# A residual-stream kernel: first residual tiles early, one weight tile in front of the gated output's loads, post-processing on two engines

## The chip, the cores and the metric

The kernel runs on one core of one Trainium2 chip. A core has a matrix engine (PE, TensorE), a vector engine (DVE), an activation engine (ACT), a general engine (POOL, GpSimd) and a queue engine (SP) that here only issues transfers; ACT issues transfers too. Each engine works through its own instructions in order. Operands live in an on-chip memory of 128 partitions (SBUF), products land in eight accumulator banks (PSUM) of 128 x 512 float32, and everything larger lies in device memory (DRAM). The metric is the device time of one execution in microseconds (us), as the median of several runs.

## What is computed

The reference is a two-layer encoder trunk on a sequence of 1024 tokens with 1024 channels, all float32:

```
for layer in range(2):
    hn = rms_norm(h, mix_norm[layer])
    h = h + (hybrid_ab_mixer(hn) if layer == 0 else rwkv7_time_mix(hn))
    h = h + swiglu(rms_norm(h, ffn_norm[layer]))
return rms_norm(h, final_norm)

swiglu(x)     = (silu(x @ w_gate) * (x @ w_up)) @ w_down     # hidden width 2816 = 22 x 128
rwkv7 step    : state = state * w_t + (state a_t) b_t + v_t k_t ;  y_t = state r_t     # 16 heads of 64
rwkv7 output  : y = groupnorm(y) * ln_w + ln_b + bonus * v ;  return (y * g) @ w_o
```

The group norm is over each head's 64 channels. The recurrence is over time and is computed in 16 chunks of 64 tokens.

## The kernel before, in words

The 1024 tokens are worked as two halves of 512 (h = 0 and h = 1), with channels on partitions: a half of the residual stream, `H[h]`, is eight k-tiles of 128 x 512. Each float32 operand is split into a rounded part and a remainder, and one product becomes three matrix instructions (`mm3`, lines 391 to 393: high x high, high x low, low x high). A weight tile is loaded into one of three `raw` buffers (line 121, issued by ACT), split by ACT (line 157) and DVE (line 158), and used. The order of the weights is fixed in a list `plan`, filled by the `push` functions; `take(key)` takes the next entry, splits it, loads the two entries behind it and splits the one behind it.

Instructions are written in program order, and a planner then orders each engine's queue by its own model of time, taking what is ready by priority. Tiles get their place in SBUF from pools that are opened and closed like a stack from two ends, left and right. A tile placed over the bytes of closed pools waits, on its first use, for the last use of the tiles that lay there.

The parts that the change touches, in order of time:

*The first layer's down projection of half 0.* The first layer's feed-forward writes its hidden tiles to DRAM (`hid_d`, line 735). For the down projection (`down_steps`, line 875) they are read back (line 886) in groups of two and three hidden tiles; for each group and each of the eight output tiles m, PE sums the group's products in one bank, and DVE adds the bank to `H[h][:, m]` (`residual`, line 485). PSUM has five banks for these products there. `H[0]` was written to DRAM (`hm_d`) in the mixer and is loaded again (line 1856), four transfers of two k-tiles for each half. The even groups' weights and hidden tiles of half 0 lie in slots cut from two activation tiles (`low_slots`, line 1827), of which k-tiles 6 and 7 are not used.

*The first recurrence, with dense work beside it.* `recur` (line 1424) computes eight chunks of half 0. A chunk (`burst`, line 1552) is a sequence of blocks of 32 small products with short DVE and ACT steps in between: a first step for the next chunk (`below`, `below2`, `own`), the product with the state, the sum Q (line 1561), the product with Q, the state's update (lines 1590 and 1591) and the output `yp`. After each second chunk `post` (line 1615) normalises 128 tokens: it copies the outputs to `ysb`, takes statistics, applies scale and shift for each head (16 ACT instructions, line 1650), multiplies by `ln_w` and adds the bonus term, for the first half of the heads on DVE and for the second on POOL (lines 1655 and 1656). `turn_out` (line 1660) transposes `ysb` on PE, multiplies by the gate on DVE (line 1672) and writes the 128 tokens to `y_d` (line 1675, SP). `drive` interleaves this with half 1's feed-forward, whose last three down groups, hidden tiles 16 and 17, 18 and 19, 20 and 21 (`steps_b`, line 1897), stand behind it in program order. Their hidden tiles have four buffers in the feed-forward's pool, and the first two groups are loaded ahead (`prime_b(2)`).

*The output projection of half 0.* While the last down group is emitted, the four pieces of the gated output are taken from `y_d` (`take_act`, line 468; ACT issues the loads). Behind them in the plan stand the eight tiles of the output weights, each loaded by four transfers; `out_proj` (line 1698) takes them one by one, 24 matrix instructions each. In the same stretch the residual stream of half 1 is normalised (line 1075) and mixed for the second half's projections, on DVE and ACT; a low-rank and a gate product follow the output projection.

## Time and profile before

| what | value |
|---|---|
| median of 3 runs | 2505.56 us (2501.13 to 2507.78) |
| the profiled execution, its own time | 2500.52 us |
| its span, first to last instruction | 2498.8 us |
| mean granted clock of PE | 0.977 |
| busy: PE, DVE, ACT, POOL | 2365.3, 1481.1, 957.6, 237.3 us |
| moved by DMA | 346.38 MB, mean 139 GB/s |

A row of the timeline gives the start in us, the duration in us, the engine, the line of the kernel, the instruction, output <- inputs by the program's names, the count of merged instructions, and in brackets how long the engine had been idle and what released it. PEld is PE's weight load, which runs under the products. SPq and ACTq are the issue of transfers, not their duration. The clock is the share of full speed that PE was granted. Matrix instructions are pipelined, so that a row's duration is longer than the distance to the next.

### The profile page before, as it was taken

What the parts mean: (1) busy time and instruction counts of PE and PEld (TensorE: products, weight loads), DVE (VectorE), ACT (ScalarE), POOL (GpSimd) and SP (SyncE); (2) the same over time, 40 slices, a digit from 0 to 9 for tenths busy, and PEclk for the clock granted to TensorE, in tenths of its full rate; (3) what the DMA queues carried; (4) which work ended last, traced back from release to release, by engine and by line L of the source; (5) the groups of instructions that cost most, each with busy time, mean ns of one, the idle gap of its engine ahead of it and who ended that gap; (6) DMA issues with size and microseconds to landing.
All of it is one profiled execution on the core that took longest, in us unless ns stands there. A gap on an engine that the chain in (4) does not pass through costs nothing. (4 is left out here: it accounts for less than half of the span.)

```text
span 2498.8 us, 38219 instructions
## 1 busy us (share of the span) xinstructions
PE 2365.3 (95%) x15519; PEld 1941.4 (78%) x15519; DVE 1481.1 (59%) x2340; ACT 957.6 (38%) x1479; POOL 237.3 (9%) x262
## 2 busy tenths in 40 slices
PE   8999999999899999989958999998999999999998
PEld 6888888888687778768846778777888778888887
DVE  6446775666467947756766847855554446444344
ACT  6233444344213644423434654432342224322223
POOL 0200000000000023301210123201110000000001
PEclk9999999999899999999978999998999999999999
DMA  5124533333765455774434465693534322433231
GB/s 175 50 68 139 159 129 120 120 120 118 251 222 206 153 165 141 217 211 134 142 128 124 145 170 140 186 238 109 142 110 143 108 80 74 152 100 114 90 95 57
DMA packets 419249, 346.38 MB, mean 139 GB/s; under 512 B 94656, under 2 KB 364096, under 8 KB 418304
## 3 DMA queue, kind: packets, MB, share of 16 engines
q10 hardware_dynamic: 264000, 193.75, 25.6%
q1 hardware_dynamic: 155072, 150.18, 19.6%
q8 instruction: 122, 2.00, 0.3%
q14 instruction: 55, 0.45, 0.1%
HBM read 264.11 MB, written 79.76 MB: 138 GB/s over the span
## 5 line engine op out<-in xcount | busy, mean ns | idle before, releaser
L391 PE MATMUL mm<-ahi,whi 128*128 128x512 f32 x1312 | 516.9, 395 | 22.8 <-ACT whi L157 21.6
L392 PE MATMUL mm<-alo,whi 128*128 128x512 f32 x1312 | 517.5, 394 | 0.1
L393 PE MATMUL mm<-ahi,wlo 128*128 128x512 f32 x1312 | 515.9, 393 | 1.4 <-DVE wlo L158 1.4
L157 ACT ACTIVATE whi<-raw 128x1024 fp32r<-128x1024 f32 (+1 forms) x276 | 274.1, 1000 | 581.6 <-PE mm L392 433.7
L158 DVE TENSOR_TENSOR wlo<-raw,whi 128x1024 fp32r<-128x1024 f32 (+1 forms) x276 | 321.9, 1169 | 213.8 <-ACT whi L157 200.8
L391 PEld LDWEIGHTS mm<-ahi,whi 128*128 128x128 f32 x1312 | 248.2, 189 | 78.9 <-ACT whi L157 24.3
L485 DVE TENSOR_TENSOR h<-h,mm 128x512 f32<-128x512 f32 x280 | 188.5, 684 | 194.4 <-PE mm L393 176.4
L393 PEld LDWEIGHTS mm<-ahi,wlo 128*128 128x128 f32 x1312 | 248.0, 189 | 55.2 <-DVE wlo L158 2.2
L392 PEld LDWEIGHTS mm<-alo,whi 128*128 128x128 f32 x1312 | 248.4, 189 | 54.2 <-issue 2.0
L391 PE MATMUL mm<-hidhi,wdhi 128*128 128x512 f32 x304 | 117.6, 397 | 5.8 <-ACT hidhi L947 2.8
L392 PE MATMUL mm<-hidlo,wdhi 128*128 128x512 f32 x304 | 119.6, 394 | 0.0
L393 PE MATMUL mm<-hidhi,wdlo 128*128 128x512 f32 x304 | 119.3, 392 | 0.0
L722 PE MATMUL mm<-ahi,whi 128*128 128x512 f32 x280 | 109.4, 391 | 0.0
L723 PE MATMUL mm<-alo,whi 128*128 128x512 f32 x280 | 109.0, 389 | 0.0
L724 PE MATMUL mm<-ahi,wlo 128*128 128x512 f32 x280 | 108.2, 389 | 0.0
L158 DVE TENSOR_TENSOR wdlo<-raw,wdhi 128x1024 fp32r<-128x1024 f32 x42 | 53.0, 1262 | 76.0 <-ACT wdhi L157 76.0
L157 ACT ACTIVATE wdhi<-raw 128x1024 fp32r<-128x1024 f32 x42 | 44.3, 1057 | 138.0 <-DMA raw<-in_ffn_w_down_dram 103.9
L944 DVE TENSOR_TENSOR sg<-sg,mm 128x512 f32<-128x512 f32 x48 | 32.9, 686 | 98.7 <-PE mm L393 98.6
L391 PE MATMUL mm<-hd,dhi 128*128 128x512 f32 x192 | 75.1, 391 | 4.1 <-DMA hd<-hid_d 2.6
L392 PE MATMUL mm<-hd,dhi 128*128 128x512 f32 x192 | 75.1, 391 | 0.0
L393 PE MATMUL mm<-hd,dlo 128*128 128x512 f32 x192 | 74.1, 389 | 0.0
L391 PEld LDWEIGHTS mm<-hidhi,wdhi 128*128 128x128 f32 x304 | 57.3, 189 | 20.8 <-DVE h L485 3.8
(395 smaller groups left out, 4457.2 us busy)
## 6 DMA issues: line engine op xcount, KB each, us to landing
raw<-in_ffn_w_down_dram ACTq DMA_DIRECT2D x88, 512.0 KB
raw<-in_ffn_w_gate_dram ACTq DMA_DIRECT2D x72, 512.0 KB
raw<-in_ffn_w_up_dram ACTq DMA_DIRECT2D x72, 512.0 KB
hid_d<-hid SPq DMA_DIRECT2D x40, 512.0 KB
hd<-hid_d SPq DMA_DIRECT2D x30, 512.0 KB
raw<-in_ab_w_in_dram ACTq DMA_DIRECT2D x16, 512.0 KB
raw<-in_ab_w_out_dram ACTq DMA_DIRECT2D x16, 512.0 KB
raw<-in_rwkv_w_r_dram ACTq DMA_DIRECT2D x16, 512.0 KB
```

What stands on the lines that cost most here:

```text
L157: act.activation(hi, src, AF.Copy)
L158: (eng or dve).tensor_tensor(out=lo, in0=src, in1=hi.bitcast(F32), op=ALU.subtract)
L391: pe.matmul(o, whi, xhi, start=first, stop=False)
L392: pe.matmul(o, whi, xlo, start=False, stop=False)
L393: pe.matmul(o, wlo, xhi, start=False, stop=last)
L485: dve.tensor_tensor(out=H[h][:, m, :], in0=H[h][:, m, :], in1=o, op=ALU.add)
L722: pe.matmul(o, wh[:, k, :], x[0][:, k, :], start=st, stop=False, skip_group_check=True)
L723: pe.matmul(o, wh[:, k, :], x[1][:, k, :], start=False, stop=False, skip_group_check=True)
L724: pe.matmul(o, wl[:, k, :], x[0][:, k, :], start=False, stop=k == 3, skip_group_check=True)
L944: dve.tensor_tensor(out=s, in0=s, in1=o, op=ALU.mult)
```

## The change

The change has three parts, all in program order and placement; the values computed are the same.

First, when the slots of `low_slots` are made, two transfers on SP load the first four k-tiles of `hm_d[0]` into the unused k-tiles 6 and 7 of both tiles. In the first down group of half 0 the add for m = 0 to 3 reads these tiles and writes `H[0]`; the loads into `H[0]` itself are now two instead of four. `H[1]` is loaded as before.

Second, the first tile of the output weights moves in the plan from behind the four pieces of the gated output to in front of them, and is taken first (`with_first`). An empty event keeps the places of the other work in that list. Along with it, half 1's hidden tiles 16 and 17 keep two buffers in the feed-forward's pool and are loaded ahead; tiles 18 to 21 get four buffers in a new pool `ffn1y`, opened on the left behind the gated output's tiles, after the recurrence's pool is closed.

Third, in `post` the scale and shift of the first half of the heads are two DVE instructions on 128 x 512 with broadcast operands instead of eight ACT instructions, and both halves' product with `ln_w` and sum with the bonus term run on DVE; the two POOL instructions are gone. This is in both recurrences, four times each.

```diff
--- before.py
+++ after.py
@@ -339,8 +339,10 @@
     for e in push_f(0, 1, D0P):
         e()
     push_d(0, 1, D0B[1])
+    o_first = push_o(0)
+    o_first[0]()
     list(push_act(("y", 0), y_d[0]))
-    push_beside(1, push_o(0) + push_f(1, 0, G1A[0]))
+    push_beside(1, [lambda: None] + o_first[1:] + push_f(1, 0, G1A[0]))
     push_proj(1, ("n1", n_d[1]))
     push_ffn(1, 0, G1A[1])
     push_ffn(1, 0, G1A[2], push_act(("y", 1), y_d[1]))
@@ -872,7 +874,7 @@
             go()
             yield 0.5
 
-    def down_steps(h, groups, wslot, hslot, ahead=True, after=None, between=iter(()), at={}):
+    def down_steps(h, groups, wslot, hslot, ahead=True, after=None, between=iter(()), at={}, first={}):
 
         held = {}
         for g in groups:
@@ -902,7 +904,10 @@
                     ms = slice(m * P, (m + 1) * P)
                     for i, f in enumerate(g):
                         mm3(o, wd[f][0][:, ms], wd[f][1][:, ms], held[f][:, 0, :], held[f][:, 1, :], i == 0, i == len(g) - 1)
-                    residual(m, h, o)
+                    if gi == 0 and m in first:
+                        dve.tensor_tensor(out=H[h][:, m, :], in0=first[m], in1=o, op=ALU.add)
+                    else:
+                        residual(m, h, o)
                     if after is not None and gi == len(groups) - 1:
                         after(m)
                     if gi == len(groups) - 1 and m % 2:
@@ -1644,16 +1649,17 @@
             rsqrt(var)
             dve.scalar_tensor_tensor(out=mean, in0=mean, scalar=-0.5, in1=var, op0=ALU.mult, op1=ALU.mult)
             yield 0.3
-            for r in range(2):
-                for p in range(8):
-                    i = r * 8 + p
-                    act.activation(
-                        ysb[:, r, p, :], ysb[:, r, p, :], AF.Identity, scale=var[:, i : i + 1], bias=mean[:, i : i + 1]
-                    )
+            vb, mb = (bc(t[:, 0:8].unsqueeze(2), [P, 8, 64]) for t in (var, mean))
+            for p in range(8):
+                act.activation(
+                    ysb[:, 1, p, :], ysb[:, 1, p, :], AF.Identity, scale=var[:, 8 + p : 9 + p], bias=mean[:, 8 + p : 9 + p]
+                )
+            dve.tensor_tensor(out=ysb[:, 0], in0=ysb[:, 0], in1=vb, op=ALU.mult)
+            dve.tensor_tensor(out=ysb[:, 0], in0=ysb[:, 0], in1=mb, op=ALU.add)
             yield 0.3
-            for q, eng in enumerate((dve, pool)):
-                eng.tensor_tensor(out=ysb[:, q], in0=ysb[:, q], in1=lnw, op=ALU.mult)
-                eng.tensor_tensor(out=ysb[:, q], in0=ysb[:, q], in1=vch[:, q], op=ALU.add)
+            for q in range(2):
+                dve.tensor_tensor(out=ysb[:, q], in0=ysb[:, q], in1=lnw, op=ALU.mult)
+                dve.tensor_tensor(out=ysb[:, q], in0=ysb[:, q], in1=vch[:, q], op=ALU.add)
             yield 0.3
 
             def turn_out():
@@ -1695,9 +1701,16 @@
         turned.pop()()
         yield 1.0
 
+    early_o = {}
+
+    def with_first(h):
+        early_o[h] = take(("o", h, 0))
+        yield from take_act(("y", h))
+
     def out_proj(h, ys, after=None):
         for m in range(KT):
-            yield from out_steps(take(("o", h, m)), ys, h, m, range(KT), after)
+            w = early_o.pop(h) if m == 0 and h in early_o else take(("o", h, m))
+            yield from out_steps(w, ys, h, m, range(KT), after)
 
     def turn(h, j):
 
@@ -1822,11 +1835,15 @@
     ps_es = open_psum("psf0", FULL)
     wp, wp_es = open_pool(name="wp", bufs=1, side="left")
 
-    low = []
+    low, first = [], {}
 
     def low_slots():
         if not low:
             low.extend(act_tiles(xlp))
+            for i, t in enumerate(low):
+                t = t[:, 6:8, :].bitcast(F32)
+                sp.dma_start(t, hm_d[0][:, 2 * i : 2 * i + 2, :])
+                first.update({2 * i + j: t[:, j, :] for j in range(2)})
         return [t[:, 2 * i : 2 * i + 2, :] for i in range(4) for t in low]
 
     lw = lambda f: [t.rearrange("p k t -> p (k t)") for t in low_slots()[2 * (f - D0A[[f in g for g in D0A].index(True)][0]) :][:2]]
@@ -1847,12 +1864,12 @@
     prime_b, steps_b = down_steps(1, D0B[0], wslot, hslot, False, lambda m: sp.dma_start(h_d[1, 0][:, m, :], H[1][:, m, :]))
     acc, add = running_sums(0)
     prime_a, steps_a = down_steps(
-        0, D0A, lambda f: (lw, wslot)[odd[f]](f), lambda f: (lh, hslot)[odd[f]](f), after=add, at={len(D0A) - 1: prime_b},
+        0, D0A, lambda f: (lw, wslot)[odd[f]](f), lambda f: (lh, hslot)[odd[f]](f), after=add, at={len(D0A) - 1: prime_b}, first=first,
     )
     prime_a()
     for h, pl in ((0, ha_pool), (1, hb_pool)):
         H[h] = pl.tile([P, KT, HT], F32, tag="h", name="h")
-        for k in range(0, KT, 2):
+        for k in range(4 * (1 - h), KT, 2):
             sp.dma_start(H[h][:, k : k + 2, :], hm_d[h][:, k : k + 2, :])
 
     def wa1():
@@ -1891,17 +1908,21 @@
     hb_pool, hb_es = open_pool(name="hb1", bufs=1, side="left")
     wp, wp_es = open_pool(name="wp0", bufs=1, side="left")
     f, f_es = open_pool(name="ffn1", bufs=1, side="right")
-    _, hslot = slots_of(f, 0, 4)
+    _, hslot = slots_of(f, 0, 2)
+    late = []
     spill_h = lambda m: sp.dma_start(h_d[1, 1][:, m, :], H[1][:, m, :])
     between = []
-    prime_b, steps_b = down_steps(1, D0B[1], lambda f: whl(), hslot, True, spill_h, (next(between[0]) for _ in range(4)))
-    prime_b(2)
+    prime_b, steps_b = down_steps(1, D0B[1], lambda f: whl(), lambda f: (hslot if f < 18 else late[0])(f), True, spill_h, (next(between[0]) for _ in range(4)))
+    prime_b()
     drive(ffn(0, 1, nxt["hn"], f, D0P, nd=2), with_reload(hb_pool, 1, h_d[1, 0], recur(0, wp)), 9.3)
     wp_es.close()
     y, y_es = open_pool(name="y0", bufs=1, side="left")
     ys = open_act(("y", 0), y)
-    between.append(take_act(("y", 0)))
+    fy, fy_es = open_pool(name="ffn1y", bufs=1, side="left")
+    late.append(slots_of(fy, 0, 4)[1])
+    between.append(with_first(0))
     drive(steps_b)
+    fy_es.close()
     f_es.close()
     ps_es.close()
     np_, np_es = open_pool(name="np1", bufs=1, side="right")
```

## The prediction, made before the changed kernel ran

> **What bounds the kernel now.** I read the page's engine shares first, then busy time by stretch, then what TensorE (PE) waited for, then the timeline around the two longest waits.
>
> ```profile
> span 2498.8 us, 38219 instructions
> PE 2365.3 (95%) x15519; PEld 1941.4 (78%) x15519; DVE 1481.1 (59%) x2340; ACT 957.6 (38%) x1479; POOL 237.3 (9%) x262
> ```
>
> PE is the bound: 133 us of the span are not PE's. No edit removes a matmul, so the change can only move PE's idle time. Stretches of the span (us, then PE, PEld, DVE, ACT, POOL busy with counts, granted clock, DMA share, GB/s):
>
> ```profile
> 624.00:636.00 12.00, 11.51 (x51) 9.13 (x50) 5.61 (x8) 4.70 (x7) 0.00 (x0) 1.00 0.98 353
> ...
> 655.70:666.90 11.20, 0.04 (x2) 0.04 (x1) 0.78 (x2) 0.00 (x0) 0.00 (x0) 0.64 0.82 271
> 666.90:673.70 6.80, 6.80 (x19) 5.38 (x20) 4.72 (x7) 0.75 (x1) 0.00 (x0) 0.59 1.00 404
> ...
> 1222.80:1278.50 55.70, 52.43 (x987) 44.08 (x985) 40.84 (x85) 21.43 (x44) 8.17 (x7) 1.00 0.42 131
> 1278.50:1323.10 44.60, 7.02 (x21) 4.35 (x20) 26.57 (x61) 19.06 (x36) 6.46 (x4) 0.56 0.41 130
> 1301.20:1370.00 68.80, 48.09 (x199) 39.09 (x200) 47.88 (x63) 34.82 (x49) 0.00 (x0) 0.81 0.54 159
> ```
>
> Two holes carry nearly half of the idle time: 11.2 us where the first half's down projection begins, and 37.6 us between the end of the first recurrence and the output projection. PE's waits in the second (total, times, longest):
>
> ```profile
> PE mm L391 <- ACT whi L157: 20.7, 2, 17.1
> PE sm L1451 <- DVE ysb L1656: 11.5, 1, 11.5
> ...
> PE sm L1451 <- ACT akv L1549: 1.4, 1, 1.4
> ```
>
> **The first hole: residual tiles.** PE fills its five accumulators and stops at 655.7; the residual add that would free one waits for H. SP's issues, PE, DVE, and what SP waited for:
>
> ```profile
> 623.41 0.32 SPq L886 DMA_DIRECT2D alo<-hid_d  x1
> ...
> 648.94 1.99 SPq L1856 DMA_DIRECT2D h<-hm_d  x4
> ...
> 659.67 1.74 SPq L1856 DMA_DIRECT2D h<-hm_d  x4
> 661.45 3.62 SPq L886 DMA_DIRECT2D hd<-hid_d  x3
> ```
>
> ```profile
> 666.87 0.80 PE L391 MATMUL mm<-ahi 128*128 128x512 f32 x1 [11.16 <-DVE h L485]
> ...
> 673.68 0.39 PE L391 MATMUL mm<-hd,dhi 128*128 128x512 f32 x1
> ...
> 685.92 0.39 PE L391 MATMUL mm<-hd,dhi 128*128 128x512 f32 x1
> ```
>
> ```profile
> 666.12 1.28 DVE L485 TENSOR_TENSOR h<-h,mm 128x512 f32<-128x512 f32 x2 [11.70 <-DMA h<-hm_d]
> ```
>
> ```profile
> SPq L1856 <- DMA hid_d<-hid: 7.4, 1, 7.4
> ```
>
> Which four loads at L1856 are H[0]'s? The second four: the add starts 6.4 us after 659.67, and these had waited 7.4 us for a hidden tile's write-out, whose space H[0] takes. The change reads the first four k-tiles from another place, loaded along with the first hidden tiles, near 623, but the add still writes into H[0], so it still needs that space, free at 659.7. So I let PE restart at 659.7 + 0.7 (one add) = 660.4, 6.5 us earlier. What is late next is the second group's hidden tiles, issued at 661.45 behind H[0]. Two loads (1.05 MB) fewer ahead of them are worth 2.6 us at the 404 GB/s of the stretch from 666.9, 3.9 us at the 271 of the one before. Bounds: 0 (they land as before, and the group starts at 673.68 again) and 6.5. I take **-5**, nearer the upper end, because at 673.68 PE waited for none of them. The two early loads fall in a stretch where DMA is 0.98 busy: 3 us more transfer there, in front of the down projection's weights, which PE first uses near 648.9 (30 products of 0.227 us, below, before 655.7). That gap hides it; without it, +3.
>
> **The second hole, as it is.** Rows of PE, ACT, DVE, POOL and SP in order:
>
> ```profile
> 1277.38 1.15 PE L1451 MATMUL yp<-uv,gt 128*64 128x64 f32 x31
> ...
> 1293.77 1.75 PE L1451 MATMUL sm<-ident,ysb 128*128 128x128 f32 x7 [3.35 <-POOL ysb L1656]
> 1295.32 1.70 PE L426 MATMUL aux<-small,nacc 128*128 128x1 f32 x8
> ...
> 1330.65 0.62 PE L393 MATMUL mm<-ahi,wlo 128*128 128x512 f32 x2
> ```
>
> ```profile
> 1285.63 5.41 ACT L1650 ACTIVATE ysb<-ysb,mean,var 128x64 f32<-128x64 f32 x16 [5.92 <-DVE mean L1645]
> 1300.42 1.30 ACTq L121 DMA_DIRECT2D raw<-y_d  x3
> 1304.40 2.25 ACT L157 ACTIVATE ahi<-raw 128x1024 fp32r<-128x1024 f32 x2 [13.36 <-DMA raw<-y_d]
> ```
>
> ```profile
> 1278.36 0.69 DVE L1591 TENSOR_TENSOR state_d<-Q,pct 128x512 f32<-128x512 f32 x1
> ...
> 1289.14 0.69 DVE L1656 TENSOR_TENSOR ysb<-ysb,vch 128x512 f32<-128x512 f32 x1
> ...
> 1301.21 4.70 DVE L1075 SCALAR_TENSOR_TENSOR hn<-h,vec,aux 128x512 f32<-128x512 f32 x7 [2.17 <-PE aux L439]
> ...
> 1316.23 1.22 DVE L158 TENSOR_TENSOR alo<-raw,ahi 128x1024 fp32r<-128x1024 f32 x1
> ```
>
> ```profile
> 1292.46 1.26 POOL L1656 TENSOR_TENSOR ysb<-ysb,vch 128x512 f32<-128x512 f32 x1
> ```
>
> The recurrence ends at 1278.5. Its last chunk pair is normalised (16 activations, then DVE, then POOL to 1293.7), turned, written and read back: y loads issue at 1300.42, the last of four pieces is split at 1317.5, and only then come the projection's first weights. Its first tile (m=0) is done at 1330.7.
>
> **Post-processing.** Activation's 16 become 8 x 0.34 = 2.7 us. DVE gets six passes of 0.72 (0.69 and the step between): two with a broadcast operand, which L1591 also has at 0.69. Four run while Activation works; the last two end 1285.6 + 4.3 = 1289.9, against POOL's 1293.7: **-3.9** in the tail. On the other seven chunk pairs DVE carries 2.9 us more each and Activation 2.7 less. Dense products hide it while PE has some; without them, +2.9 a pair if DVE's queue decides, -1.4 if Activation's does (the akv wait above). I take 0.
>
> **The late hidden tiles.** Tiles 18 to 21 now go to a pool in the space of the recurrence's tiles, so they load when it ends, and their 96 products can no longer run under it. Behind the waiting loads on SP stand the other half's spills and y's last write, all due later. How much of them ran there:
>
> ```profile
> L391 PE MATMUL mm<-hd,whi 128*128 128x512 f32 x33 | 13.6, 411 | 0.0
> ```
>
> 33 triples (99 products) after 1222.8: all of it. One product takes 0.227 us (54 from 673.68 to 685.92), so 21.8 us move from a stretch that is 94% busy into one that is 84% idle. What does the recurrence do without them? Its chunks (the product with Q, the next chunk's first step, and that step's bare sequence early on):
>
> ```profile
> 1108.35 0.69 PE L1451 MATMUL sm<-XT,gt 32*32 32x32 f32 x32
> ...
> 1111.53 0.98 PE L1451 MATMUL sm<-state_d,ar 64*64 64x64 f32 x27
> ...
> 1126.08 1.72 PE L1451 MATMUL sm<-Q,XT 64*64 64x64 f32 x32
> ```
>
> ```profile
> 1229.70 1.11 PE L1451 MATMUL sm<-Q,XT 64*64 64x64 f32 x32
> ...
> 1235.58 0.69 PE L1451 MATMUL sm<-XT,gt 32*32 32x32 f32 x32
> ...
> 1250.17 1.15 PE L1451 MATMUL sm<-Q,XT 64*64 64x64 f32 x32 [0.28 <-DVE Q L1561]
> ...
> 1273.43 1.15 PE L1451 MATMUL sm<-Q,XT 64*64 64x64 f32 x32
> ```
>
> The last two chunks took 20.5 and 23.3 us. Bare: 5.9 to the next step (1229.70 to 1235.58), 4.2 for it (1108.35 to 1112.5), about 1.2 for the add of Q: 11.3. I take 15.5, nearer the bare chain, since DVE and Activation still carry the post-processing. Two chunks give 12.8, the one before 2.2: the recurrence ends 15 us earlier, at **1263.5**. Bounds 0 and 21.8 (all of the products).
>
> Then, in order: the tiles land 4.0 after the release (as y did, 1300.42 to 1304.40), 1267.5; 96 products and 2.4 of transposes end at 1291.7. The y chain took 21.9 from the recurrence's end to its loads; now 18.0 and 1.0 for residual adds on the same DVE, 1282.5; plus 17.0 for the last split, 1299.5.
>
> **First weights in front.** Four DMAs on Activation's queue, one activation (1.05) and one DVE pass (1.22) move ahead of the y loads, under the last down products; uncovered, 2.3. The second weights take the place the first had. So m=0 runs as the pieces come, done 1.4 after the last: 1300.9 against 1330.7, **-29.8** with the two edits above.
>
> **What is late next.** The other half's norm needs the late groups' sums: 1291.7 + 2 + 5.9 (1295.32 to 1301.21) = 1299.6, hardly earlier than 1301.21. From there to 1370 DVE has 47.9 us of work, 43 without the y splits, now partly before; the projection's other seven tiles need 7 x 24 x 0.227 = 38.1 and end at 1339, but the low-rank and gate products want that DVE work, 1342.6. So about **+4**.
>
> Sum: -5 - 29.8 + 4 = -30.8. The profiled execution took 2500.52 (1.7 beside the span), the runs' median is 2505.56; off the median, **2474.8, so 2475**.
>
> **Rivals.**
>
> *The recurrence keeps its pace.* Thin PE work lets the clock fall: early on, at 1126.08, the product with Q took 1.72 instead of 1.11, as L391's took 0.80 after the first hole instead of 0.39. With eleven blocks of about 1 us a chunk, 0.55 each is 6 us: 15.5 becomes 21.5. Against it: 15.5 leaves only some 4.5 us of waits a chunk, spread over several places. If it comes, the recurrence ends at 1278.5, m=0 at 1316, the norm starts at 1314.6 and DVE holds the gate to 1357.6 instead of 1354: -14.7 + 4 - 5, 2490. The Trainium skill, "TensorE: Matmul & The Clock Gate", Part 1, has PE throttled only after about 3.4 us without work; by that rule this rival would not come, and the trace's clock of 0.64 in the 11.2 us hole agrees that long holes do it.
>
> *Slower: the late loads queue behind the y write-out.* SP works in order. If the four loads stand behind the last write of y, which cannot issue before 1293, and the recurrence keeps its pace, the groups run from 1297 to 1321 (2.4 more at half clock), the norm starts at 1331, and the gate's operands are there at 1331 + 48 = 1379 against 1369: +10 - 5, 2511. The planner issues what its own clock has ready, and the release comes 15 us before the write, which speaks against.
>
> *Everything at its bound.* Chunks at 11.3, 21.8 won, m=0 at 1294, +3.6 after, and -8 in front (6.5 and a shorter cold spell): 2464.
>
> *It doesn't do what it says.* A planned order that changes elsewhere by as much, or late tiles lying over space freed only by the post-processing: 2503.
>
> **Numbers.** Forecast 0.58, pace kept 0.16, at the bounds 0.12, nothing 0.07, slower 0.07. A measurement here tells about 0.3% (7.5 us) from no change: faster 0.85, same 0.08, slower 0.07. Range 2458 to 2498; the forecast's own 2464 to 2486.
>
> **What would show it.** PE restarting near 660 with the add no longer waiting for H; products on tiles 18 to 21 after the recurrence's last product and before the y loads' split; that last product near 1263 less the front's gain; transposes right behind DVE, not POOL; m=0 done some 30 us earlier against the same point, and a new wait for DVE before the gate. It is wrong if the recurrence ends as late as now, or if the loads of tiles 18 to 21 come after the last write of y.

## The result, and the profile after

The changed kernel takes 2478.39 us (median; 2476.45 to 2481.59) against 2503.97 for the kernel before: a ratio of 0.9905, 95% interval 0.989 to 0.992, or 25.6 us less. The profiled execution took 2477.8 us, its span 2476.1 against 2498.8. The head of the page and its engine shares:

```profile
span 2476.1 us, 38179 instructions
...
PE 2371.4 (96%) x15519; PEld 1948.0 (79%) x15519; DVE 1496.4 (60%) x2372; ACT 937.6 (38%) x1415; POOL 215.5 (9%) x246
```

PE's products are the same in number; its idle time went from 133.5 us to 104.7, and 6.1 us of that came back as longer products. DVE has 15 us more work, ACT 20 less, POOL 22 less. To see where the time went, the span is cut at two products that both kernels have. The first is the start of the second down group, 673.68 in the prediction's rows; the other is the first product of the second recurrence. The kernel before, timeline of PE:

```profile
1318.24 0.80 PE L391 MATMUL mm<-ahi,whi 128*128 128x512 f32 x1 [17.07 <-ACT whi L157]
...
1652.80 0.29 PE L1453 MATMUL sm<-ar,bk 64*64 64x128 f32 x1 [0.60 <-DMA bk<-bk_d]
```

The kernel after, the same products:

```profile
665.26 0.47 PE L393 MATMUL mm<-hd,dhi 128*128 128x512 f32 x1
...
1307.37 0.39 PE L393 MATMUL mm<-ahi,whi 128*128 128x512 f32 x1
...
1641.07 0.32 PE L1458 MATMUL sm<-ar,bk 64*64 64x128 f32 x1
```

Up to the second down group 8.4 us were won (673.68 - 665.26). From there to the second recurrence the two kernels take 979.1 and 975.8 us: 3.3 won, where the prediction had 25.8. From there to the end of the span they take 846.0 and 835.0: 11.0 won, where it had nothing. Together that is 22.7 us, for this one pair of executions; the medians are 25.6 apart, since the profiled execution of the kernel before lay below its median.

**The first hole.** After, SP, DVE and PE:

```profile
658.46 0.80 SPq L1873 DMA_DIRECT2D h<-hm_d  x2
```

```profile
658.52 1.28 DVE L908 TENSOR_TENSOR h<-ahi,mm 128x512 f32<-128x512 f32 x2 [7.89 <-DMA hid_d<-hid]
```

```profile
659.26 0.50 PE L393 MATMUL mm<-ahi 128*128 128x512 f32 x1 [4.72 <-DVE h L908]
```

The add now waits for the write-out of a hidden tile, whose space H[0] takes, and no longer for H[0]'s loads. PE is back at 659.26, and the second group (665.26) waits for nothing.

**The first recurrence, its tail, and the projection.** After, the product with Q and the last output of the recurrence on PE, then the tail:

```profile
1220.08 1.09 PE L1456 MATMUL sm<-Q,XT 64*64 64x64 f32 x32
...
1236.21 1.63 PE L1456 MATMUL sm<-Q,XT 64*64 64x64 f32 x32 [2.43 <-DVE Q L1566]
...
1252.47 1.98 PE L1456 MATMUL sm<-Q,XT 64*64 64x64 f32 x32 [0.94 <-DVE Q L1566]
...
1257.53 1.10 PE L1456 MATMUL yp<-uv,gt 128*64 128x64 f32 x32
...
1268.63 0.45 PE L1456 MATMUL sm<-ident,ysb 128*128 128x128 f32 x1 [10.00 <-DVE ysb L1662]
...
1279.56 0.80 PE L393 MATMUL mm<-hd,whi 128*128 128x512 f32 x1 [7.05 <-DMA hd<-hid_d]
```

What SP waited for after 1255, and what it issued then:

```profile
SPq L1681 <- DVE gch L1678: 19.2, 1, 19.2
```

```profile
1273.88 0.53 SPq L1681 DMA_DIRECT2D y_d<-gch  x1
1274.51 2.72 SPq L888 DMA_DIRECT2D hd<-hid_d  x4
```

The recurrence ends at 1258.6 instead of 1278.5. But the late hidden tiles' space is free then, and their loads are issued only at 1274.51: they stand on SP behind the last write of the gated output, for which SP waits 19.2 us. PE stands still for 10.0 us before the transposes and 7.05 after them, works on the late products from 1279.56 to 1307.4, and starts the projection there.

**The second recurrence.** Here nothing but the post-processing was edited. Two windows, each at the same distance from this recurrence's first product in both kernels (it is 11.73 us earlier in the kernel after), before and then after (us, then PE, PEld, DVE, ACT, POOL busy, clock, DMA share, GB/s):

```profile
1640.00:1720.00 80.00, 74.21 (x1042) 61.16 (x1041) 35.68 (x68) 22.26 (x38) 6.06 (x6) 0.96 0.76 192
1720.00:1760.00 40.00, 30.73 (x402) 25.19 (x402) 22.02 (x32) 14.20 (x26) 5.10 (x5) 0.83 0.50 144
```

```profile
1628.27:1708.27 80.00, 74.80 (x1049) 61.19 (x1048) 40.80 (x77) 23.29 (x40) 6.28 (x6) 0.98 0.74 192
1708.27:1748.27 40.00, 37.65 (x636) 31.12 (x635) 23.80 (x55) 13.41 (x21) 3.15 (x5) 0.96 0.58 170
```

Before, PE is idle for 9.3 of the 40 us of the second window, after for 2.4. The rows of that hole before, on PE, DVE and ACT:

```profile
1736.52 1.97 PE L1451 MATMUL sm<-ident,bk 128*128 128x128 f32 x8 [4.88 <-DVE gt L1498]
1742.27 1.12 PE L1451 MATMUL sm<-ident,ysb 128*128 128x128 f32 x4 [3.78 <-DVE Q L1590]
```

```profile
1732.91 2.83 DVE L158 TENSOR_TENSOR wdlo<-raw,wdhi 128x1024 fp32r<-128x1024 f32 x1 [3.72 <-ACT wdhi L157]
1735.77 1.29 DVE L1498 TENSOR_TENSOR gt<-sm,gm 128x512 f32<-128x512 f32 x2
...
1740.39 1.23 DVE L158 TENSOR_TENSOR wdlo<-raw,wdhi 128x1024 fp32r<-128x1024 f32 x1 [3.33 <-ACT wdhi L157]
1741.53 0.68 DVE L1590 TENSOR_TENSOR Q<-S,sm 128x512 f32<-128x512 f32 x1
```

```profile
1731.83 1.06 ACT L157 ACTIVATE wdhi<-raw 128x1024 fp32r<-128x1024 f32 x1 [4.13 <-DMA raw<-in_ffn_w_down_dram]
```

Twice the split of a down weight stands in DVE's queue ahead of a step of the recurrence (gt, then Q), and DVE waits for that weight while PE waits for the step. What ends last is the weight's transfer (the ACT row), not an instruction of post-processing, and it holds PE up because the planner's order has the split in front. Whether the hole shrank by post-processing or by another order is not settled: over the same 40 us PE is idle for 6.5 to 10.2 us in the seven kernels below without the whole third part, and for 1.9 to 6.4 in the seven with it.

### The profile page after: what moved, and what is told of

It reads as the page before. It is cut to its first block, busy times and chain, and to the rows that moved or that the text cites. A ratio compares the mean times of both kernels' runs of the same rounds, so it can differ in the third digit from the quotient of the medians.

```text
span 2476.1 us, 38179 instructions
## 1 busy us (share of the span) xinstructions
PE 2371.4 (96%) x15519; PEld 1948.0 (79%) x15519; DVE 1496.4 (60%) x2372; ACT 937.6 (38%) x1415; POOL 215.5 (9%) x246
```

## The experiments

All comparisons are with the kernel before on the same chip; the table cuts each profiled span at the same places as above. "Group 2" is the start of the second down group, "R1 ends" the end of the first recurrence's last output, "projection" its first product, "R2 starts" the second recurrence's first product, "rest" the span from there to its end.

| kernel | ratio, 95% interval | group 2 | R1 ends | projection | R2 starts | rest |
|---|---|---|---|---|---|---|
| before | 1 | 673.68 | 1278.5 | 1318.2 | 1652.8 | 846.0 |
| the change | 0.9905, 0.989 to 0.992 | 665.26 | 1258.6 | 1307.4 | 1641.1 | 835.0 |
| first tiles alone | 0.9956, 0.9945 to 0.9968 | 666.30 | 1271.8 | 1311.0 | 1646.3 | 842.3 |
| post-processing alone | 0.9945, 0.9932 to 0.9958 | 672.87 | 1278.2 | 1316.6 | 1654.3 | 837.4 |
| late tiles alone | 0.9968, 0.9958 to 0.9979 | 671.82 | 1269.0 | 1320.3 | 1653.7 | 842.5 |
| first weights alone | 0.9943, 0.9929 to 0.9957 | 673.17 | 1274.0 | 1301.3 | 1641.6 | 839.3 |
| first tiles and post | 0.9916, 0.9902 to 0.993 | 665.34 | 1269.2 | 1305.5 | 1642.3 | 837.2 |
| all but the late tiles | 0.9893, 0.9879 to 0.9908 | 666.11 | 1271.3 | 1295.4 | 1637.1 | 842.7 |
| all, half the late tiles | 0.9897, 0.9882 to 0.9912 | 665.50 | 1263.6 | 1298.9 | 1634.8 | 838.3 |
| all, last write on ACT | 0.992, 0.9907 to 0.9933 | 664.82 | 1258.8 | 1306.1 | 1640.6 | 839.6 |
| half late, write on ACT | 0.9919, 0.9904 to 0.9933 | 666.78 | 1264.6 | 1298.7 | 1639.1 | 838.9 |
| scale and shift alone | 0.9979, 0.997 to 0.9988 | 670.19 | 1275.9 | 1315.9 | 1652.8 | 843.6 |
| ln_w and bonus alone | 0.9963, 0.9949 to 0.9978 | 674.27 | 1276.5 | 1314.6 | 1651.6 | 840.5 |
| control | 0.9988, 0.9976 to 1.0001 | 671.50 | 1277.0 | 1317.4 | 1651.0 | 849.1 |

The times of a row are from one execution. The kernels without the first tiles differ by up to 4 us at "group 2", and kernels with the same queues in the second recurrence by 3 in "rest"; differences smaller than that are not read. The executions of this table also lie off their medians, most of all that of first weights alone (6.3 us below) and that of all but the late tiles (4.6 above).

### Each part alone

First tiles alone:

```diff
-    low = []
+    low, first = [], {}
...
+            for i, t in enumerate(low):
+                t = t[:, 6:8, :].bitcast(F32)
+                sp.dma_start(t, hm_d[0][:, 2 * i : 2 * i + 2, :])
+                first.update({2 * i + j: t[:, j, :] for j in range(2)})
...
-        for k in range(0, KT, 2):
+        for k in range(4 * (1 - h), KT, 2):
```

> The kernel before with the first part alone (early residual tiles). My theory: in the changed kernel PE restarted at 659.26 and the second group began at 665.26 without a wait, against 673.68 before, 8.4 us, of which about 1.2 us were there already at the loads into the other half's tiles (647.77 against 648.94) and belong to the start of the program. So this part alone should be worth 7 to 8.5 us, about 2496.5, and the whole offset should stand from 666 to the end. Rival: the later stretch gives the 7 us back (the planner orders the rest anew, or a later wait ends at a fixed time), 2500 to 2504, with the offset seen at 666 and gone at the first recurrence.

It took 2492.35 against 2503.23, 10.9 us less. The offset at the second group (-7.4) is still there at the second recurrence (-6.5), so it isn't given back. The rest of the gain lies in "rest" (846.0 to 842.3), where this part edits nothing: a first sign that the second recurrence gains from something else.

Post-processing alone:

```diff
-            for r in range(2):
-                for p in range(8):
...
+            dve.tensor_tensor(out=ysb[:, 0], in0=ysb[:, 0], in1=vb, op=ALU.mult)
+            dve.tensor_tensor(out=ysb[:, 0], in0=ysb[:, 0], in1=mb, op=ALU.add)
...
-            for q, eng in enumerate((dve, pool)):
+            for q in range(2):
```

> The kernel before with the third part alone (post-processing on DVE and ACT). My theory, from the trace of the changed kernel: from the end of the first recurrence to the last normalised tile 12.0 us instead of 15.2, so -3 in that tail; and in the second recurrence, where neither of the other parts changes anything, the changed kernel won a further 10 us between 1640 and 1760, because products that waited for the operands gt and Q (11.0 and 3.8 us) waited less. If that is this part's doing, the sum is -13, about 2491. Rival one: the second recurrence's 10 us come from another order of the weights (their plan is shifted by the other parts), then -3, about 2501. Rival two: as I had predicted, DVE carries 2.9 us more for each chunk pair and that shows where its queue decides: 0 or slower, 2504 to 2510.

2490.38 against 2503.23, 12.9 us less, as the first theory had it. All of it lies in "rest" (846.0 to 837.4); up to the second recurrence the kernel is not faster at all (1654.3 against 1652.8). The -3 in the first tail does not reach the second recurrence.

Late tiles alone:

```diff
-    _, hslot = slots_of(f, 0, 4)
+    _, hslot = slots_of(f, 0, 2)
+    late = []
...
+    fy, fy_es = open_pool(name="ffn1y", bufs=1, side="left")
+    late.append(slots_of(fy, 0, 4)[1])
```

> The kernel before with the move of hidden tiles 18 to 21 alone: their 96 products behind the first recurrence; the output projection's first weights stay behind the gated output's loads, post-processing and residual tiles as before. My theory: the recurrence ends 10 to 12 us earlier (about 1267 against 1278.5), the four loads stand on SP behind the last write of the gated output, PE stands still for about 20 us and the late products then run while the gated output is read back and split; the projection's first tile is done 10 to 12 us earlier than at 1330.7, and about 4 to 8 us are left at the end: about 2498. Rival one: without the first weights in front the projection starts when the late products have ended and its weights have come, nothing is won, 2504. Rival two: the products behind the recurrence cost more than the recurrence gains (PE idle for 20 us and 21.8 us of products), 2510.

2495.75 against 2503.23, 7.5 us less. The recurrence does end 9.6 us earlier, but the projection starts 2.1 later and the second recurrence 0.9 later: up to there the move is worth nothing. PE's waits between 1260 and 1340 (total, times, longest) show what took the place of the 17.1 us for the weights:

```profile
PE sm L1451 <- DVE ysb L1656: 11.5, 1, 11.5
PE mm L391 <- DMA hd<-hid_d: 7.0, 1, 7.0
PE sm L1451 <- POOL ysb L1656: 3.3, 1, 3.3
```

First weights alone:

```diff
-    list(push_act(("y", 0), y_d[0]))
-    push_beside(1, push_o(0) + push_f(1, 0, G1A[0]))
+    o_first = push_o(0)
+    o_first[0]()
+    list(push_act(("y", 0), y_d[0]))
+    push_beside(1, [lambda: None] + o_first[1:] + push_f(1, 0, G1A[0]))
...
-    between.append(take_act(("y", 0)))
+    between.append(with_first(0))
```

> The kernel before with only the output projection's first weights taken in front of the gated output's loads. On top of the first and the third part this had been worth 6.7 us (2483.9 to 2477.2). Theory: the wait of 17.1 us for those weights' split shrinks to the wait for the gated output's pieces whatever else is changed, 6 to 8 us, 2496 to 2498. Rival: without the other parts the four transfers and the split stand on ACT in front of the 16 post-processing instructions and delay the gated output by the 2 to 3 us that I had put down as the uncovered price, 2500 to 2506.

2489.0 against 2502.61, 13.6 us less, more than either expectation. The projection starts 17 us earlier (12.4 counted from the recurrence's end) and the second recurrence 11.2 earlier; "rest" gains too (839.3). The profiled execution was its fastest (2482.70), so that part of these offsets is scatter. PE's waits from 1260 to 1340:

```profile
PE sm L1453 <- DVE ysb L1658: 11.7, 1, 11.7
PE mm L393 <- ACT ahi L157: 4.8, 2, 4.4
PE mm L393 <- ACT whi L157: 3.9, 2, 2.3
```

The wait of 17.1 us for the first weights has become 4.4 for the first piece of the gated output and 3.9 for the second and third weights.

The four parts alone add up to 10.9 + 12.9 + 7.5 + 13.6 = 44.9 us; together they bring 25.6. Something is counted more than once. In the table's columns the four parts won 15.3 us up to the second recurrence, against 11.7 for the change, and 22.5 in "rest", against 11.0: most of the excess lies in "rest". The control below is about that.

### Parts together

First tiles and post-processing:

> The kernel before with the first part and the third (early residual tiles, post-processing on DVE and ACT); hidden tiles 18 to 21 and the output projection's first weights stay as they were. Alone the two had brought 10.9 and 12.9 us. Theory: they act in different stretches and add up, 2503 - 24 = 2479, which is what the whole change reaches, so that the moved hidden tiles and the weights in front, to which my prediction gave 26 of its 31 us, are worth next to nothing on top. Rival: part of both is the same rearrangement of the second recurrence and counts once, 2486 to 2490, and the second part brings the remaining 8 to 10 us.

2483.91 against 2503.87, 20 us less: neither the sum (24) nor the rival's 15. At the second recurrence the front's gain is there (-10.6, of which 8.3 at the second group), and "rest" is that of post-processing alone.

All but the late tiles; the changed kernel with that part undone:

```diff
-    _, hslot = slots_of(f, 0, 2)
-    late = []
+    _, hslot = slots_of(f, 0, 4)
...
-    prime_b()
+    prime_b(2)
```

> The changed kernel with hidden tiles 18 to 21 put back under the first recurrence (four buffers in the feed-forward's pool, two groups loaded ahead); the output projection's first weights stay in front of the gated output's loads. Theory: the wait of 17.1 us for those weights' split (16.4 with the third part alone) shrinks to the wait for the gated output's last split, near 1316 less the front's 8 us, and the recurrence keeps its dense work: PE's hole between recurrence and projection is then some 25 us instead of 38, without the late products' costs, 2479 - 12 = about 2467, a version better than the change. Rival: what is won at the projection's first tile is lost to the norm of the other half on DVE (43 us of work before the gate's products), 2476 to 2480.

2477.24 against 2503.87, 26.6 us less: as fast as the whole change. So the late tiles, to which the prediction gave most of its gain, bring nothing measurable on top of the others. Up to the second recurrence this kernel is ahead of the change by 4.0 us (1637.1 against 1641.1), though not at the end: "rest" takes 842.7, with the same edits there as in the change, where it takes 835.0; some of this may be the execution, which was 4.6 us above its median. Its first projection tile ends where the wait for the second weights begins (1307.60 less 2.07):

```profile
1295.44 0.80 PE L393 MATMUL mm<-ahi,whi 128*128 128x512 f32 x1 [4.33 <-ACT ahi L157]
...
1307.60 0.50 PE L393 MATMUL mm<-ahi,whi 128*128 128x512 f32 x1 [2.07 <-ACT whi L157]
```

That is 1305.5; with the late tiles it is 1307.37 + 24 x 0.227 = 1312.8.

### The late tiles' queue

The changed kernel with one write moved off SP:

```diff
-                sp.dma_start(y_d[h][:, :, jj * P : (jj + 1) * P], gch)
+                (act if h == 0 and jj == 3 else sp).dma_start(y_d[h][:, :, jj * P : (jj + 1) * P], gch)
```

> The changed kernel, with the last write of the first half's gated output issued by ACT instead of SP, so that on SP the loads of hidden tiles 18 to 21 stand behind nothing but the end of the recurrence. Theory: the price of the queue on SP is what I had named in the slower rival; the loads then issue at about 1259 instead of 1274.5, land at about 1263, PE runs the late products from there instead of from 1279.6, and the splits of the gated output, whose load buffers come free with those products, end some 12 us earlier: about 2466 to 2468. Rival: the chain of the gated output (normalised tiles, transposes, write, read back, split) sets the projection's start whatever the late products do, and the transposes now stand among the products on PE: 2474 to 2479, the late products early and PE idle behind them instead.

2484.43 against 2503.23, 18.8 us less: no gain over the change (25.6 us less; the intervals overlap). SP, PE and DVE:

```profile
1254.45 5.57 SPq L888 DMA_DIRECT2D hd<-hid_d  x4
```

```profile
1268.73 0.45 PE L1456 MATMUL sm<-ident,ysb 128*128 128x128 f32 x1 [9.99 <-DVE ysb L1662]
...
1272.26 0.78 PE L393 MATMUL mm<-hd,whi 128*128 128x512 f32 x1
...
1284.41 0.79 PE L393 MATMUL mm<-hd,whi 128*128 128x512 f32 x1 [5.67 <-DVE h L487]
```

```profile
1282.53 1.23 DVE L158 TENSOR_TENSOR alo<-raw,ahi 128x1024 fp32r<-128x1024 f32 x1 [8.58 <-ACT ahi L157]
1283.68 1.88 DVE L487 TENSOR_TENSOR h<-h,mm 128x512 f32<-128x512 f32 x3
```

The loads are 20 us earlier (1254.45 against 1274.51), and the hole only moves twice. PE's queue has the transposes in front of the late products, so PE still waits 9.99 us for post-processing. Then the products fill the free accumulators and stop for 5.67 us, since DVE's queue has the first split of the gated output in front of the residual adds that would free one. The projection starts at 1306.1, 1.3 us earlier than in the change. The queue on SP was therefore a wait that ended last, but with two others close behind it. In the profiled executions this kernel is 4.1 us behind the change, and that arises after the second recurrence's start (839.6 against 835.0), where the code is the same and some twenty instructions of DVE's queue stand in other places.

Half of the late tiles:

```diff
-    _, hslot = slots_of(f, 0, 2)
+    _, hslot = slots_of(f, 0, 4)
...
-    prime_b, steps_b = down_steps(1, D0B[1], lambda f: whl(), lambda f: (hslot if f < 18 else late[0])(f), True, spill_h, (next(between[0]) for _ in range(4)))
-    prime_b()
+    prime_b, steps_b = down_steps(1, D0B[1], lambda f: whl(), lambda f: (hslot if f < 20 else late[0])(f), True, spill_h, (next(between[0]) for _ in range(4)))
+    prime_b(2)
...
-    late.append(slots_of(fy, 0, 4)[1])
+    late.append(slots_of(fy, 0, 2)[1])
```

> The changed kernel with only the last two hidden tiles (20 and 21, 48 products) behind the recurrence; 18 and 19 go back under it. With all four behind it PE had 21.5 us of waits between the recurrence and the projection and the recurrence itself ran thin (its waits 19.4 us, the product with Q at 1.63 to 1.98 us instead of 1.15); with none (the run before) 25 us of waits until the projection's third product. Theory: half of them fills the hole that is left and lets the recurrence keep the other half, so that the section up to the second recurrence ends 4 to 8 us earlier than with all or none; the second recurrence, whose stretch to the end took 835 to 843 us in kernels with the same post-processing, may give or take 4: 2468 to 2475. Rival: the loads stand behind the last write on SP here too, so the products run from about 1280 on beside a projection that could start at 1295, and it is a wash: 2475 to 2480.

2476.01 against 2502.61, 26.6 us less, the best median, yet not to be told from the change or from the kernel without late tiles. The second recurrence starts 6.2 us earlier than in the change, which is the gain that was expected of this section, and "rest" takes 838.3.

Half of the late tiles, and the write on ACT:

> As the run before, with the last write of the gated output issued by ACT, so that the two hidden tiles load as soon as the recurrence ends. With all four tiles this had PE work some 7 us earlier (1272 instead of 1279.6) and then stand still for 5.7 us, because DVE's queue had the first split of the gated output in front of the residual adds. With 48 products in five or six accumulators that stall has less behind it. Theory: 3 to 5 us better than the run before, 2465 to 2472. Rival: the stall on DVE stays and nothing is gained, within 2 us of the run before.

2482.46 against 2502.61, 20.1 us less, slower than the run before. The wait for the loads (7.0 us there) is gone; the stall on DVE has grown from 4.7 to 7.1 at its longest and from 5.7 to 11.8 in all:

```profile
PE mm L393 <- DVE h L487: 11.8, 2, 7.1
```

### Post-processing, by halves

Scale and shift on DVE, POOL's two passes kept:

```diff
-            for q in range(2):
-                dve.tensor_tensor(out=ysb[:, q], in0=ysb[:, q], in1=lnw, op=ALU.mult)
+            for q, eng in enumerate((dve, pool)):
+                eng.tensor_tensor(out=ysb[:, q], in0=ysb[:, q], in1=lnw, op=ALU.mult)
...
```

(The lines are shown against the whole third part, not against the kernel before.)

> The kernel before with one half of the third part: scale and shift of the first eight heads are two DVE instructions instead of eight of ACT; POOL keeps its two passes on the second half. The third part as a whole had brought 12.9 us, 8.5 of them in the second recurrence's profile. Theory: it is ACT's 5.4 us block of 16 instructions, behind which the splits of the weights stand, so this half brings nearly all of it: 2491 to 2494. Rival: it is POOL's two passes, beside which DVE's instructions ran longer in the kernel before (1.71 us and, beside the other POOL pass, 2.83 us instead of 1.23): then this half brings 0 to 4, 2499 to 2503.

2499.51 against 2503.87, 4.4 us less.

ACT's 16 instructions kept, POOL's two passes on DVE:

> The kernel before with the other half of the third part: the product with ln_w and the bonus sum of the second eight heads run on DVE instead of POOL; ACT keeps its 16 instructions. By the theory that ACT's block costs the time, this brings 1 to 3 us in the first recurrence's tail and nothing else: 2500 to 2503. By the rival (POOL's passes slow DVE down and end last), it brings 8 to 12: 2491 to 2495. If both halves bring much less than 12.9 together, the gain is one of the order of the queues and belongs to neither.

2495.34 against 2503.87, 8.5 us less. The halves add up to 12.9, the whole part's gain, and the larger half is POOL's, against my theory. But their "rest" columns (843.6 and 840.5) are no further from the kernel before than those of kernels that don't touch post-processing there (842.3, 842.5, 839.3). So these two don't show what POOL's passes or ACT's block cost in themselves.

### A control for the second recurrence

Two of the kernels above, late tiles alone and first weights alone, have the second recurrence's code unchanged, and from its start on have the queues in the same order as one another (three pairs of neighbours apart), though not in that of the kernel before. Is the kernel before's order a slow one? The control is the kernel before with the write on ACT; from the second recurrence on its queues are exactly those of the kernel before.

> A control: the kernel before, with the last write of the first half's gated output issued by ACT instead of SP. Every engine's queue is that of the kernel before except for this one issue, from the second recurrence on without any difference. In the profiles the stretch from the second recurrence's first product to the end took 846.0 us in the kernel before, and 835.0 to 843.6 in all eleven other kernels, also in the two whose code for it is unchanged and whose queues are in another order there (842.5 and 839.3). Theory: the order that the planner made for the kernel before is the slow one, so this profile shows 845 to 847 again and the median stays at 2501 to 2505. Rival: 846.0 was one slow execution, the stretch takes 838 to 843 here too, and the gain of the other kernels in it is theirs.

2501.59 against 2504.8, a ratio of 0.9988 that includes 1. "Rest" took 849.1 us, 2 more than the theory's upper end and far from the rival's 838 to 843. The two waits are there again at their places:

```profile
1735.50 1.97 PE L1451 MATMUL sm<-ident,bk 128*128 128x128 f32 x8 [4.42 <-DVE gt L1498]
1742.60 0.69 PE L1451 MATMUL sm<-ident,ysb 128*128 128x128 f32 x2 [5.13 <-DVE Q L1590]
```

So the slow "rest" belongs to the order that the planner had made for the kernel before, and not to one execution: 846.0 and 849.1, mean 847.5. Other orders of the same code took 842.3, 842.5 and 839.3, mean 841.4, some 6 us less. The medians bear this out: by them these three kernels gained 4.4, 8.4 and 2.4 us more than the start of their second recurrence had moved. With the whole third part "rest" is 835.0 to 842.7 in seven kernels, mean 838.4, some 3 us less again, with a spread of nearly 8 between orders and executions.

What makes that order slow? It is not the two waits alone. Over the 40 us at the same distance from the second recurrence's start PE is idle for 9.3 us in the kernel before and 10.2 in the control, but also for 8.5, 6.8 and 6.9 in late tiles alone, first weights alone and first tiles alone. There too DVE waits for the splits of the down weights; the first one stands in front of another step (uv). The windows over all of "rest", in the kernel before, the control and first weights alone (columns as above):

```profile
1652.80:2498.80 846.00, 814.67 (x5797) 672.01 (x5797) 400.41 (x598) 259.29 (x403) 51.23 (x45) 0.98 0.38 112
```

```profile
1650.97:2500.10 849.13, 815.36 (x5797) 672.87 (x5797) 399.55 (x598) 259.06 (x403) 51.91 (x45) 0.98 0.38 112
```

```profile
1641.61:2480.95 839.34, 810.40 (x5798) 668.57 (x5797) 399.80 (x598) 259.35 (x403) 51.15 (x45) 0.99 0.38 113
```

PE's products, the same number, take 814.7 and 815.4 us in the old order, and 810.4, 811.0 and 812.7 in the three others: 3.6 less in the mean. Its idle time is 31.3 and 33.8 against 28.9, 31.5 and 29.6: 2.5 less. So more than half of the 6 us are longer products, at a lower granted clock: in the 40 us above it was 0.83 and 0.83 against 0.96, 0.91 and 0.87. Which of the moved instructions bring that about stays open.

Each of the four parts alone made the planner choose anew, and may have collected these 6 us; together they collect them once. Counted four times, that is 18 too many, and 44.9 - 18 = 26.9 is near the 25.6 of the whole. This is an estimate from single executions: in the table's columns the excess in "rest" is 11.5.

## Why the prediction was right in its sum, and where its steps were not

The forecast was 2475 and the result 2478.39, with a sum of -30.8 against -25.6. That it came out near was luck: its largest term, with what follows it, was forecast at -25.8 and is -3.3 between the same products, and 11 us came from a place to which it gave nothing. By the prediction's own sign ("if the loads of tiles 18 to 21 come after the last write of y") its account of the second hole was wrong. One reading was loose as well: the two holes carry 48.8 of 133.5 us of idle time, 37% and not nearly half.

- **First hole, -5 (bounds 0 and 6.5).** The mechanism is right in each step: H[0]'s space decides, PE restarts at 659.26 where 660.4 was worked out, and the second group's loads don't hold it up. Over seven kernels with this part the second group starts at 665.7 on average, over seven without it at 672.5: -6.8. The mis-sized term is the wait for those loads, which I let cost 1.5 us and which is nothing.
- **Post-processing in the tail, -3.9.** The last normalised tile is ready 12.0 us after the recurrence (1258.6 to 1270.6) instead of 15.2: -3.2. Right in kind and nearly in size, but by itself it brought nothing to the second recurrence's start.
- **Post-processing elsewhere, 0.** Right for the first recurrence. In the second it is about -3 by the means of "rest", the part that goes beyond a new order; no run separates it from the order that comes with it.
- **Late tiles: the recurrence 15 us shorter.** It ends 19.9 us earlier, 11.5 without the front's 8.4. Its chunks took 16.1 and 16.3 us between products with Q (1220.08, 1236.21, 1252.47) where 15.5 was worked out. Near with the other parts; alone, the late tiles shorten the stretch from the second group to the recurrence's end by 7.7.
- **Late tiles: m=0 done 29.8 us earlier.** This is the step that failed. It was 1312.8 against 1330.7: 17.9 earlier, and 9.5 without the front. It rested on "the tiles land 4.0 after the release", 1267.5, and on their products being done at 1291.7. They ran from 1279.56 to 1307.4, and the projection, whose operands had been split by 1304.0, started behind them. The loads were issued behind the last write of the gated output, as my slower rival had it; I had set that aside with the argument that the planner issues what its own clock has ready and that the release comes 15 us before the write. What counts is that the write stands first in SP's queue; how long after the release it comes only sets the price. The rival's price was wrong as well, since it let the recurrence keep its pace. And the experiment with the write on ACT shows that the step would have failed without that queue too: PE's and DVE's own orders put the late products behind post-processing and the first split.
- **First weights in front.** I had folded them into the same -29.8. They are what works there: alone they move the projection's start by 17 us, on top of the first and third parts by 10.0 (1305.5 to 1295.4), and with the late tiles undone m=0 ends 7.3 us earlier than in the change.
- **What is late next, +4.** From m=0's end to the second recurrence the change takes 1641.1 - 1312.8 = 328.3 us against 322.1: +6.2. In kind as predicted, somewhat larger.
- **The second recurrence, nothing.** It won 11.0 us: some 6 by a new order and 3 by post-processing, going by the means above; the remainder is within the spread. In these two executions 7.0 of the 11.0 are idle time of PE and 4.0 are shorter products. The prediction had looked for this part's costs in ACT's and DVE's time and not at whose instruction stands ahead of whose.

The rival in which the recurrence keeps its pace did not come, though the clock of which it spoke did fall in the bare chunks (0.58 and 0.67, below).

Open is which orders are good in the second recurrence, and why: the kernel with the earliest start there (1634.8) and the one with the shortest rest (835.0) are not the same, and no run joined them.

## What to carry to other kernels

Where a planner orders the queues, an edit also pays or collects what a new order of everything behind it is worth: 3.5, 3.7 and 6.7 us here, from three edits that touch nothing in the stretch where they won it. Cut the spans at products that both kernels have, and credit an edit with the section that it touches; a control with unchanged queues tells a slow old order from one slow execution. Before a wait is named as the cost of an order, look for it in the faster orders too. Before moving work into a hole, name for every queue it passes (the loads' issue, the matrix engine, the engine that frees the accumulators) what stands in front of it there.

## What the runs showed of the hardware that was not expected

**The clock falls without a long wait.** After, two windows of the bare chunks (us, then PE, PEld, DVE, ACT, POOL busy, clock, DMA share, GB/s):

```profile
1230.00:1240.00 10.00, 7.57 (x162) 7.36 (x162) 7.02 (x12) 3.95 (x10) 2.35 (x1) 0.67 0.15 55
1250.00:1258.60 8.60, 7.66 (x162) 7.28 (x154) 2.20 (x4) 1.19 (x2) 0.00 (x0) 0.58 0.22 65
```

The granted clock is 0.67 and 0.58, and the products with Q in these windows took 1.63 and 1.98 us instead of 1.09. The longest wait in the first window is 2.43 us, in the second 0.94, and between 1205 and the recurrence's end PE never waits longer than 2.74. The rule that the prediction drew from the Trainium skill, "TensorE: Matmul & The Clock Gate", Part 1 (PE is throttled after about 3.4 us without work), would not have it; the measurement decides. The Trainium skill, "TensorE: Matmul & The Clock Gate", section "A second HAM failure mode: psum-queue depth-cycling", tells of another kernel in which frequent short idle times between groups of products made the clock swing between half and full. The trace agrees with that in kind.

**Of a DVE split and a POOL pass, the one that starts second pays.** Before, in the hole of the second recurrence, the split of a down weight at 1732.91 took 2.83 us, and the same split at 1740.39 took 1.23. Beside the first ran one POOL pass (and in its last microsecond two memsets):

```profile
1732.76 1.90 POOL L1630 TENSOR_TENSOR vch<-vch,bon 128x1024 f32<-128x1024 f32 x1 [7.17 <-DMA vch<-v_d]
```

The Trainium skill, "SBUF — State Buffer", section "Who interferes with whom", says that a DVE instruction with two inputs in SBUF contends with a GpSimd instruction that reads SBUF, through a shared read port. The two rows agree: 1.60 us more, where POOL's pass has 1.75 us left when the split starts. Two other runs show the reverse order. In first weights alone the split starts first, by 0.02 us:

```profile
1723.66 1.23 DVE L158 TENSOR_TENSOR wdlo<-raw,wdhi 128x1024 fp32r<-128x1024 f32 x1 [4.14 <-ACT wdhi L157]
```

```profile
1723.68 2.96 POOL L1632 TENSOR_TENSOR vch<-vch,bon 128x1024 f32<-128x1024 f32 x1 [7.04 <-DMA vch<-v_d]
```

The split takes its 1.23 us and the pass 2.96 instead of 1.90. In the control the split starts 0.37 us ahead of the pass; it takes 1.23 us again, and the pass 2.61.
